# Sums of weight blocks: from VectorE in the down-projection to accumulating DMAs in DRAM

## The chip, the core and the metric

The kernel runs on one core of a Trainium2 chip. A core has five engines that work side by side, each through its own queue in order: PE (TensorE, matrix products), PEld (the weight loads of PE, which overlap its products), DVE (VectorE), ACT (ScalarE) and POOL (GpSimd); SP (SyncE) computes nothing and issues most of the DMAs. Sixteen DMA engines move data between DRAM (HBM) and the on-chip memory SBUF, or from DRAM to DRAM. Products land in PSUM, from where ACT or DVE copy them out. Engines wait for each other and for DMAs by semaphores.

The metric is the device time of one execution in microseconds (us); lower is better.

## What is computed

One step of a one-layer encoder on 1056 rows (1024 prompt rows and 32 sample rows) of 1024 features, all in float32. Cut to what matters:

```python
def layer(x, p, attend, conv_buf, g_mix, w_in, conv_w, w_attn_out, w_conv_out, w_o,
          g_ffn, w_up, w_down, g_ple, w_ple_gate, w_ple):
    h = rmsnorm(x, g_mix)
    proj = h @ w_in                                   # 1024 -> 5120: the input stage
    q, k, v, cb, cc, cx, ga, gc = jnp.split(proj, SPLITS, axis=-1)
    y_attn = attend(q, k, v).reshape(b, t, SB_WIDTH) @ w_attn_out
    conv_out, new_buf = causal_conv(cc * cx, conv_buf, conv_w)
    y_conv = (cb * conv_out) @ w_conv_out
    merged = jax.nn.sigmoid(ga) * y_attn + jax.nn.sigmoid(gc) * y_conv
    x = x + merged @ w_o
    f = jnp.square(jax.nn.relu(rmsnorm(x, g_ffn) @ w_up)) @ w_down    # up, then down
    x = x + f
    x = x + jax.nn.sigmoid(rmsnorm(x, g_ple) @ w_ple_gate) * (p @ w_ple)
```

`w_down` is 4096 x 1024. The change touches how its blocks are prepared.

## The kernel before

**Stages.** The work runs in order: input projection (from the start to about 429 us), attention with small projections filled in, branch outputs and `w_o`, up-projection (to about 1075 us), down-projection (about 1075 to 1405 us), and the gate of the per-layer embedding with the final norm. Activations are held with features on the 128 partitions and rows along the free dimension.

**Products.** Every float32 operand is split into a high part, rounded to the float32r format of TensorE, and the low remainder; a product is three matmuls (high by high, high by low, low by high). The high part of a weight block is a cast on ACT, the low part a subtraction on DVE.

**Seven products in place of eight.** The large projections use the Strassen-Winograd scheme on 2 x 2 blocks: from the weight blocks A11, A12, A21, A22 come S1 = A21 + A22, S2 = S1 - A11, S3 = A11 - A21 and S4 = A12 - S2; from the activation blocks come T1 to T4; seven block products and some additions of results give the four output blocks.

**The input stage.** After the first gates, which use plain products, sets of two output blocks are worked on in pairs (`seven_pair`, 25 steps of 12 or more matmuls each, eight pairs). Between steps, `run` lets every generator in the list `side` advance once: these load the weights of the next sets (SP queue, four buffers), sum their blocks on POOL (`prepare`, L228, and `prepare_inner`), cast the high parts on ACT (L167), subtract the low parts on DVE (L226), and finish the results of earlier sets (scales, sigmoids, stores to DRAM). ACT copies most products out of PSUM: the copies named `u_i` (L491), `s_i` (L486) and `p_i` (L481) must be made before PE can go on in the same PSUM bank. The order on ACT, PE, DVE and POOL is the order in which the code issues the instructions. `after(n, ...)` holds a generator back for n steps.

**The down-projection.** 56 units: two halves c of the 4096 inputs, in each the seven products P1, P2, P5, P6, P7, P4, P3 in that order, in each product four column pairs n2. One unit is 48 matmuls. Weights come as 128 x 1024 blocks (0.5 MB) by SP (`fetch_w`, L1704) three units ahead; activation operands by `fetch_mid` six units ahead. `sum_w` makes S1 (P5), S2 (P6), S3 (P7) and S4 (P3) on DVE two units ahead of their use: at L1732 for P5 and P6, at L1727 for P7, at L1730 for P3; P1, P2 and P4 use blocks of `w_down` as they are. For S1 and S3 two blocks are loaded instead of one (the second into the tile `sw` for P5, into a second `raw_dn` buffer for P7). S1 is kept in `sw` and turned into S2 and then used for S4. `high_w` (ACT, L1737) and `low_w` (DVE, L1743) then split the block. The products of a unit are L1850 to L1852; DVE and ACT add them out of PSUM at L1854 to L1864.

Of the kernel before, what the change touches and what calls it, by code (L numbers as in the profile page):

```python
# [9 lines left out]
F32 = mybir.dt.float32  # L10
# [5 lines left out]
P = 128  # L16
D = 1024
KD = D // P
SEQ = 1024
DEC = 32  # L20
T = SEQ + DEC
# [19 lines left out]
RAW_GATES = 6  # L41
ORDER = "LSAFBFG"
LAG = 2
START = 0.33
BP = (8, 9)
TAIL = 0
# [5 lines left out]
def tile_step(  # L52
# [8 lines left out]
    nc = tc.nc  # L61
# [3 lines left out]
    wraw = ctx.enter_context(tc.tile_pool(name="wraw", bufs=RB))  # L65
    wsp = ctx.enter_context(tc.tile_pool(name="wsp", bufs=2))
    dpool = ctx.enter_context(tc.tile_pool(name="dpool", bufs=1, space=bass.MemoryType.DRAM))

    def blk(name, dt=F32, shape=None):
        return bpool.tile(shape or [P, T], dt, tag="B", name=name)  # L70
# [58 lines left out]
    add, sub = ALU.add, ALU.subtract  # L129
    dve, pool = nc.vector.tensor_tensor, nc.gpsimd.tensor_tensor  # L130
    raws, ws, side = {}, {}, []
# [428 lines left out]
    def after(n, *gens):  # L560
        for _ in range(n):
            yield
        for g in gens:
            yield from g

    def call(f, *a):
        f(*a)
        yield
# [187 lines left out]
    NSET = DFF // (2 * P)  # L756
    NCH = 2
    NP_ = NSET // NCH
# [11 lines left out]
    cvd = dpool.tile([4, 2, P, T], F32, name="cvd")  # L770
    ed = dpool.tile([KD, P, T], F32, name="ed")
    edt = dpool.tile([P, 2, 2 * P], F32, name="edt")
    oT = []
    ch, cl = [], []
    st, cst = {}, {}
# [534 lines left out]
    with tc.manual_schedule(engines=MM):  # L1310
        nc.scalar.preload_act_table_set("sqrt_and_others")
        run(first_gates())
        side.append(after(1, stats_x()))
        side.extend(ahead_of("i", 3, 3))
        side.append(after(5, inner_operands("x", gmix, lambda to, f: nc.sync.dma_start(to, xf[f][:, :TH]))))
        m = blk("m1_i2"), blk("m2_i2")
        run(seven("i2", *m, copy_of))
        follow(*SETS[2], m)
        last_ = len(SETS) - 1
        for a in range(3, last_, 2):  # L1320
            more = a + 2 < last_
            pair_side("i", a, a + 1, in_pair(a + 2, a + 3) if more else None)
            if not more:
                side.extend([after(15, low_parts()), after(8, call(fetch_in, last_)), after(12, prepare(f"i{last_}", (6, 8, 10, 12, 15, 17)))])
            run(input_pair(a, a + 1))
        m = blk(f"m1_i{last_}"), blk(f"m2_i{last_}")
        side.append(after(2, call(p_fetch), call(keys_values, 0, 0), call(queries, 0, 0, 0), call(queries, 0, 0, 1), call(queries, 0, 0, 2), call(queries, 0, 0, 3)))
        side.append(after(8, *(call(p_parts, f) for f in range(2)), *(call(embed_weights, i) for i in range(2))))
        side.append(after(9, call(next, work)))
        run(seven(f"i{last_}", *m, copy_of))  # L1330
        follow(*SETS[last_], m)
        run(ahead(START))
        while side:
            run(range(1))
# [68 lines left out]
    def pace():  # L1403
# [6 lines left out]
        load, own = [], []  # L1410
        for n in range(ns + LAG):
            a, b, c = size(n - 1), size(n - LAG), size(n - LAG - 1)
# [15 lines left out]
    with tc.manual_schedule(engines=MM):  # L1428
        next(sample)
        for n in range(len(steps) + LAG + 1):  # L1430
            done_f, parts = 0, None
            w0, w1 = (pace_ + [FILL])[n : n + 2]
            if n < len(steps):
                i = steps[n][2]
# [8 lines left out]
            for op in ORDER:  # L1443
# [9 lines left out]
                elif op == "G" and n > LAG and steps[n - LAG - 1][2] % 2 == 1:  # L1453
                    p, j, i_ = steps[n - LAG - 1]
# [231 lines left out]
    def up_source(a, b):  # L1686
# [3 lines left out]
    SEVEN = (  # L1690
        ("P1", "A11", "B11"), ("P2", "A12", "B21"), ("P5", "S1", "T1"), ("P6", "S2", "T2"),
        ("P7", "S3", "T3"), ("P4", "A22", "T4"), ("P3", "S4", "B22"),
    )
    ND = NCH * 7 * 4
    dws, opd, mraw, sw, dt_ = {}, {}, {}, {}, {}

    def unit(u):
        c, r = divmod(u, 28)
        i, n2 = divmod(r, 4)
        return c, i, n2  # L1700

    def quarter_w(to, a, b, c, n2):
        n = 2 * n2 + a
        nc.sync.dma_start(to, w_down[n, b][:, c * NP_ : (c + 1) * NP_, :])  # L1704

    def fetch_w(u):
        c, i, n2 = unit(u)
        k = SEVEN[i][0]
        raw = dws[u] = wraw.tile([P, NP_, P], F32, tag="raw", name=f"raw_dn{u}")
        a, b = {"P2": (0, 1), "P5": (1, 1), "P4": (1, 1), "P3": (0, 1)}.get(k, (0, 0))  # L1710
        quarter_w(raw, a, b, c, n2)
        if k == "P5":
            sw[n2] = swp.tile([P, T], F32, tag="sw", name=f"sw{u}")
            quarter_w(sw[n2][:, : NP_ * P].rearrange("p (k n) -> p k n", n=P), 1, 0, c, n2)
        elif k == "P7":
            dws[u] = raw, wraw.tile([P, NP_, P], F32, tag="raw", name=f"raw_dn{u}b")
            quarter_w(dws[u][1], 1, 0, c, n2)

    def sum_w(u):

        c, i, n2 = unit(u)
        k, raw = SEVEN[i][0], dws[u]
        if k in ("P1", "P4", "P2"):
            return
        s = sw[n2][:, : NP_ * P].rearrange("p (k n) -> p k n", n=P)
        if k == "P7":
            dve(raw[0], raw[0], raw[1], op=sub)  # L1727
            dws[u] = raw[0]
        elif k == "P3":
            dve(raw, s, raw, op=sub)  # L1730
        else:
            dve(s, s, raw, op=add if k == "P5" else sub)  # L1732
            dws[u] = s

    def high_w(u):
        hi = wsp.tile([P, NP_, P], F32R, tag="whi", name=f"whi_dn{u}")
# [32 lines left out]
    def held(k, n2):  # L1769
        return dt_[k][n2 // 2][:, n2 % 2, :]  # L1770
# [57 lines left out]
    def down_unit(u):  # L1828
        c, i, n2 = unit(u)
        k = SEVEN[i][0]  # L1830
        hi, lo = dws.pop(u)
        ops = [opd[(c * 7 + i) * 4 + j] for j in range(NP_ // 2)]
        e = None

        ends = {"P2": (0, 0), "P7": (1, 1), "P4": (1, 0), "P3": (0, 1)}.get(k)
        if ends:
            n, h = 2 * n2 + ends[0], ends[1]
            e = fetch_x(c, n, h)
        if k in ("P1", "P5", "P6"):
            d = state({"P1": "b1", "P5": "b5", "P6": "b6"}[k], n2)  # L1840
        elif k in ("P2", "P7"):
            d = dp.tile([P, TH], F32, tag="e", name=f"c{u}", bufs=EB)
        else:
            d = held({"P4": "b6", "P3": "b5"}[k], n2)
        for t in range(2):
            ps = group(f"ps_dn{u}_{t}", TQ)
            q = quarters[t]
            for j in range(NP_):
                oh, ol = (o[:, j % 2, q] for o in ops[j // 2])
                nc.tensor.matmul(ps, hi[:, j, :], oh, start=j == 0, stop=False)  # L1850
                nc.tensor.matmul(ps, hi[:, j, :], ol, start=False, stop=False)  # L1851
                nc.tensor.matmul(ps, lo[:, j, :], oh, start=False, stop=j == NP_ - 1)  # L1852
            if k in ("P1", "P5"):
                nc.scalar.copy(d[:, q], ps)  # L1854
            elif k in ("P2", "P6"):
                dve(d[:, q], ps, held("b1", n2)[:, q], op=add)
            elif k == "P7":
                b6 = held("b6", n2)[:, q]
                dve(d[:, q], ps, held("b5", n2)[:, q], op=add)  # L1859
                dve(b6, ps, b6, op=add)  # L1860
            elif k == "P4":
                dve(d[:, q], ps, d[:, q], op=add)
            else:
                dve(d[:, q], d[:, q], ps, op=sub)  # L1864
            yield
        if k == "P6":
            b5 = held("b5", n2)
            later.append(partial(dve, b5, d, b5, op=sub))
        if ends:
            into_x(c, n, h, d, e)  # L1870
# [261 lines left out]
    with tc.manual_schedule(engines=MM):  # L2132
# [36 lines left out]
        swp = ctx.enter_context(tc.tile_pool(name="swp", bufs=4))  # L2169
# [4 lines left out]
        for u in range(ND):  # L2174
            v = u + 4
            if u + 1 < ND:
                high_w(u + 1)
            else:
                ple_high(0)
            if v < ND:  # L2180
                high_mid(v)
            if u + 2 < ND:
                sum_w(u + 2)
            if u + 1 < ND:
                low_w(u + 1)
            else:
                ple_low(0)
            body = down_unit(u)
            if u + 3 < ND:
                fetch_w(u + 3)  # L2190
            else:
                ple_fetch(u + 3 - ND)
            if v + 2 < ND:
                fetch_mid(v + 2)
            if u == LASTP:
                nc.scalar.preload_act_table_set("sqrt_and_others")
                later.extend(partial(norm_late, n, halves[0]) for n in (1, 3, 5, 7, 0, 2, 4, 6))
                seen["rs3"], seen["ssq3"] = blk("rs3"), blk("ssq3")
            settle(2 + (u < ND - 1) if u >= LASTP else 1)
            next(body)  # L2200
            if v < ND:
                low_mid(v)
            settle(2 + (u < ND - 1) if u >= LASTP else 1)
            for _ in body:
                pass
# [9 lines left out]
        for t in (1, 2):  # L2215
            ps = rows_of([seen["ssq2"][:, tt[t]]], t, f"ps_n{t}")
# [109 lines left out]
```

## Time and profile before

| | |
|---|---|
| median of 3 runs | 1518.92 us (1518.25 to 1519.84) |
| the profiled execution | 1519.13 us |
| its span, from the first to the last instruction | 1517.4 us |
| granted TensorE clock, mean of the span | 0.998 of full speed |
| busy: PE, PEld, DVE, ACT, POOL | 99%, 98%, 76%, 52%, 28% of the span |
| moved by DMA | 270.47 MB, mean 178 GB/s |

How to read the views that follow: a group of instructions is given by line, engine, operation, the tiles it writes and reads (`out<-in`), its shape and count, then its busy time in us, the mean of one in ns and the idle time of the engine just before. A row of waits says which instruction of which engine waited for which other, in total, how often, and the longest, all in us. A row of a stretch gives its length and for each engine the busy us in it (and how many instructions), the granted clock, the share of the 16 DMA engines that was busy and the rate. A row by tile has least, median and most ns, and the first and the last start in us. Matmuls are pipelined and their ends are modelled. Idle time of an engine that is not the bottleneck costs nothing.

### The profile page before, as it was taken

The page shows a single profiled execution, that of the slowest core. Times are in us where ns is not written, and L with a number is a line of the kernel's source. Part 1 is how long each engine was busy: PE and PEld are TensorE (multiplying, and loading weights), DVE is VectorE, ACT ScalarE, POOL GpSimd, SP SyncE. Part 2 cuts the span into 40 slices and gives each one's busy share as a digit, 9 for nine tenths or more (in the row PEclk, how much of TensorE's full clock was granted, in tenths as well). Part 3 has the DMA queues.
Part 4 walks back from the last instruction along what each step waited for, and adds up shares of the span by engine and source line. Part 5 has one row for each costly group of instructions (what it writes and reads, how often), then busy time and mean ns, then how long its engine had stood idle before and what let it go on. Part 6 is the DMA issues. An engine that isn't in the chain of part 4 may idle for free.

```text
span 1517.4 us, 29531 instructions
## 1 busy us (share of the span) xinstructions
PE 1496.5 (99%) x11600; PEld 1483.4 (98%) x11600; DVE 1154.7 (76%) x1567; ACT 785.1 (52%) x1549; POOL 430.7 (28%) x362
## 2 busy tenths in 40 slices
PE   8999999999999999999999999999999999999997
PEld 8999999999999999999999999999999999999997
DVE  7667688879578989876786586666687977789856
ACT  6654444445467667433475555555543334444656
POOL 1233334444121211003324343332020221012453
PEclk9999999999999999999999999999999999999999
DMA  6624425422677432545644434444986897583443
GB/s 244 211 71 169 163 63 197 155 84 96 221 254 249 131 110 78 208 173 193 230 139 156 143 130 147 145 154 160 349 282 203 270 336 250 192 276 106 147 131 114
DMA packets 116746, 270.47 MB, mean 178 GB/s; under 512 B 14048, under 2 KB 30048, under 8 KB 116608
## 3 DMA queue, kind: packets, MB, share of 16 engines
q1 hardware_dynamic: 115888, 266.40, 51.9%
q8 instruction: 91, 1.49, 0.4%
q10 hardware_dynamic: 720, 2.19, 0.4%
q14 instruction: 47, 0.39, 0.1%
HBM read 187.81 MB, written 80.73 MB: 177 GB/s over the span
## 4 chain that ended last, share of the span: by engine, by line
PE 93%; DVE 3%; ACT 2%; issue 1%; DMA 1%; SPq 0%; DVEq 0%; ACTq 0%
PE ps_dn L1852 7%; PE ps_dn L1851 7%; PE ps_dn L1850 7%; PE ps_A11i L347 4%; PE ps_A11i L348 4%; PE ps_A11i L349 4%; PE ps_A11u L348 4%; PE ps_A11u L347 4%; PE ps_A11u L349 4%; PE av L1199 2%; PE ps_wo L111 2%; PE ps_wo L110 2%; PE ps_wo L109 2%; PE ps_S1i L348 2%; PE ps_S1i L349 2%; PE ps_S1i L347 2%
## 5 line engine op out<-in xcount | busy, mean ns | idle before, releaser
L1852 PE MATMUL ps_dn<-fh,wlo_dn 128*128 128x264 f32 x896 | 255.2, 285 | 0.0
L1851 PE MATMUL ps_dn<-fl,whi_dn 128*128 128x264 f32 x896 | 254.7, 284 | 0.2 <-DVE fl L1759 0.2
L1850 PE MATMUL ps_dn<-fh,whi_dn 128*128 128x264 f32 x896 | 254.8, 284 | 0.0
L1851 PEld LDWEIGHTS ps_dn<-fl,whi_dn 128*128 128x128 f32 x896 | 168.6, 188 | 0.4 <-DVE fl L1759 0.4
L1852 PEld LDWEIGHTS ps_dn<-fh,wlo_dn 128*128 128x128 f32 x896 | 168.5, 188 | 0.2 <-DVE wlo_dn L1743 0.2
L1850 PEld LDWEIGHTS ps_dn<-fh,whi_dn 128*128 128x128 f32 x896 | 168.7, 188 | 0.0
L1792 POOL TENSOR_TENSOR c<-c,ssq 128x528 f32<-128x528 f32 x16 | 26.4, 1652 | 242.6 <-DVE c L1859 122.5
L1737 ACT CAST whi_dn<-raw_dn 128x1024 fp32r<-128x1024 f32 x40 | 42.1, 1052 | 94.0 <-PE ps_dn L1851 79.7
L1144 DVE TENSOR_TENSOR_SCAN r<-r 128x128 f32<-128x128 f32 (+3 forms) x64 | 86.7, 1355 | 4.8 <-POOL r L1137 4.8
L1743 DVE TENSOR_TENSOR wlo_dn<-raw_dn,whi_dn 128x1024 fp32r<-128x1024 f32 x40 | 71.0, 1776 | 24.0 <-ACT whi_dn L1737 23.5
L347 PE MATMUL ps_A11i<-T,shS_i 128*128 128x264 f32 x288 | 82.5, 287 | 1.6 <-ACT u_i L491 1.6
L348 PE MATMUL ps_A11i<-T,shS_i 128*128 128x264 f32 x288 | 82.1, 285 | 0.0
L349 PE MATMUL ps_A11i<-T,slS_i 128*128 128x264 f32 x288 | 81.9, 284 | 0.0
L1137 POOL TENSOR_SCALAR_AFFINE_SELECT r<-r 128x128 f32<-128x128 f32 x64 | 34.1, 533 | 139.6 <-ACT r L1130 139.5
L347 PE MATMUL ps_A11u<-T,shS_u 128*128 128x264 f32 x256 | 73.1, 286 | 0.0
L348 PE MATMUL ps_A11u<-T,shS_u 128*128 128x264 f32 x256 | 72.9, 285 | 0.0
L349 PE MATMUL ps_A11u<-T,slS_u 128*128 128x264 f32 x256 | 72.8, 285 | 0.0
L1759 DVE TENSOR_TENSOR fl<-mr,fh 128x1056 fp32r<-128x1056 f32 x56 | 69.7, 1247 | 3.8 <-ACT fh L1754 3.8
L1754 ACT CAST fh<-mr 128x1056 fp32r<-128x1056 f32 x56 | 59.9, 1074 | 5.8 <-DMA mr<-mdB 5.8
L111 PE MATMUL ps_wo<-mh,wlo_wo 128*128 128x352 f32 x192 | 62.1, 323 | 0.0
L110 PE MATMUL ps_wo<-ml,whi_wo 128*128 128x352 f32 x192 | 62.0, 323 | 0.0
L109 PE MATMUL ps_wo<-mh,whi_wo 128*128 128x352 f32 x192 | 61.5, 323 | 0.0
(1652 smaller groups left out, 5622.6 us busy)
## 6 DMA issues: line engine op xcount, KB each, us to landing
raw_dn<-in_w_down_dram SPq DMA_DIRECT2D x56, 512.0 KB, 4.9
mr<-mdT SPq DMA_DIRECT2D x32, 528.0 KB, 5.6
mdB<-m SPq DMA_DIRECT2D x48, 264.0 KB, 2.1
mr<-mdB SPq DMA_DIRECT2D x24, 528.0 KB, 6.6
s<-gd SPq DMA_DIRECT2D x16, 528.0 KB, 5.2
mdT<-ta SPq DMA_DIRECT2D x32, 264.0 KB, 3.2
raw_pg<-in_w_ple_gate_dram SPq DMA_DIRECT2D x15, 512.0 KB, 3.5
gd<-m_i SPq DMA_DIRECT2D x12, 528.0 KB, 3.0
```

What stands on the lines that cost most here:

```text
L109: nc.tensor.matmul(ps, wh, xh[k][:, cols], start=(k == order[0]), stop=False)
L110: nc.tensor.matmul(ps, wh, xl[k][:, cols], start=False, stop=False)
L111: nc.tensor.matmul(ps, wl, xh[k][:, cols], start=False, stop=(k == order[-1]))
L347: nc.tensor.matmul(p_, wh[:, k, :], h, start=new and n == 0, stop=False, **on)
L348: nc.tensor.matmul(p_, wh[:, k, :], l, start=False, stop=False, **on)
L349: nc.tensor.matmul(p_, wl[:, k, :], h, start=False, stop=z, **on)
L1144: nc.vector.tensor_tensor_scan(rev, rev, rev, 1.0, ALU.mult, ALU.bypass)
L1743: dve(lo, raw, hi.bitcast(F32), op=sub)
L1759: dve(l, mraw.pop(v), opd[v].bitcast(F32), op=sub)
L1850: nc.tensor.matmul(ps, hi[:, j, :], oh, start=j == 0, stop=False)
L1851: nc.tensor.matmul(ps, hi[:, j, :], ol, start=False, stop=False)
L1852: nc.tensor.matmul(ps, lo[:, j, :], oh, start=False, stop=j == NP_ - 1)
```

## The change

The four sums of blocks of `w_down` are made in DRAM, in 16 new tensors `dsum` of 1 MiB (four sums by four column pairs, both halves c at once). A generator `down_sums` joins the list `side` after the first gates and starts 16 steps later. For each column pair it copies a block of `w_down` into the tensor, DRAM to DRAM, by a DMA that ACT issues, and adds another block, or an earlier sum, by an accumulating DMA that POOL issues. [...] Between copy and addition lie 8 steps, in all 40 steps for a column pair and 160 for four; one column pair is worked on after the other.

In the down-projection `sum_w` and its 32 subtractions and additions are gone, and so are the second loads for P5 and P7 (16 loads of 0.5 MB); `fetch_w` reads the finished sum for P5, P6, P7 and P3.

```diff
+SPACE = 8
+DS0 = 16
...
+    dsum = {k: [dpool.tile([P, NSET, P], F32, name=f"ds{k}{n}") for n in range(KD // 2)] for k in ("S1", "S2", "S3", "S4")}
+
+    def down_sums():
+
+        def copy(k, n, a, b):
+            nc.scalar.dma_start(dsum[k][n], w_down[2 * n + a, b])
+
+        def plus(k, n, src):
+            nc.gpsimd.dma_start(dsum[k][n], src, accum_op=add, max_dma_last_dim=4096)
+
+        for n in range(KD // 2):
+            copy("S1", n, 1, 0)
+            yield from after(SPACE)
+            copy("S3", n, 0, 0)
+            plus("S1", n, w_down[2 * n + 1, 1])
+            yield from after(SPACE)
+            copy("S2", n, 0, 0)
+            plus("S3", n, w_down[2 * n + 1, 0])
+            yield from after(SPACE)
+            copy("S4", n, 0, 1)
+            plus("S2", n, dsum["S1"][n])
+            yield from after(2 * SPACE)
+            plus("S4", n, dsum["S2"][n])
...
         side.append(after(5, inner_operands("x", gmix, lambda to, f: nc.sync.dma_start(to, xf[f][:, :TH]))))
+        side.append(after(DS0, down_sums()))
         m = blk("m1_i2"), blk("m2_i2")
...
     def fetch_w(u):
         c, i, n2 = unit(u)
-        k = SEVEN[i][0]
+        k = SEVEN[i][1]
         raw = dws[u] = wraw.tile([P, NP_, P], F32, tag="raw", name=f"raw_dn{u}")
-        a, b = {"P2": (0, 1), "P5": (1, 1), "P4": (1, 1), "P3": (0, 1)}.get(k, (0, 0))
-        quarter_w(raw, a, b, c, n2)
-        if k == "P5":
-            sw[n2] = swp.tile([P, T], F32, tag="sw", name=f"sw{u}")
-            quarter_w(sw[n2][:, : NP_ * P].rearrange("p (k n) -> p k n", n=P), 1, 0, c, n2)
-        elif k == "P7":
-            dws[u] = raw, wraw.tile([P, NP_, P], F32, tag="raw", name=f"raw_dn{u}b")
-            quarter_w(dws[u][1], 1, 0, c, n2)
-
-    def sum_w(u):
-        ...
+        src = dsum[k][n2] if k in dsum else w_down[2 * n2 + int(k[1]) - 1, int(k[2]) - 1]
+        nc.sync.dma_start(raw, src[:, c * NP_ : (c + 1) * NP_, :])
...
             elif k in ("P2", "P6"):
-                dve(d[:, q], ps, held("b1", n2)[:, q], op=add)
+                dve(d[:, q], ps, held("b1", n2)[:, q], op=add if k == "P2" else sub)
             elif k == "P7":
                 b6 = held("b6", n2)[:, q]
-                dve(d[:, q], ps, held("b5", n2)[:, q], op=add)
-                dve(b6, ps, b6, op=add)
+                dve(d[:, q], held("b5", n2)[:, q], ps, op=sub)
+                dve(b6, b6, ps, op=sub)
...
             else:
-                dve(d[:, q], d[:, q], ps, op=sub)
+                dve(d[:, q], ps, d[:, q], op=sub)
...
-            if u + 2 < ND:
-                sum_w(u + 2)
```

More of the change, by code (lines that the diff above doesn't have):

```diff
@@ L1694, in tile_step @@
     ND = NCH * 7 * 4
-    dws, opd, mraw, sw, dt_ = {}, {}, {}, {}, {}
+    dws, opd, mraw, dt_ = {}, {}, {}, {}
     def unit(u):
@@ L1700, in unit @@
         return c, i, n2
-    def quarter_w(to, a, b, c, n2):
-        n = 2 * n2 + a
-        nc.sync.dma_start(to, w_down[n, b][:, c * NP_ : (c + 1) * NP_, :])
     def fetch_w(u):
         c, i, n2 = unit(u)
-        k = SEVEN[i][0]
+        k = SEVEN[i][1]
         raw = dws[u] = wraw.tile([P, NP_, P], F32, tag="raw", name=f"raw_dn{u}")
-        a, b = {"P2": (0, 1), "P5": (1, 1), "P4": (1, 1), "P3": (0, 1)}.get(k, (0, 0))
-        quarter_w(raw, a, b, c, n2)
-        if k == "P5":
-            sw[n2] = swp.tile([P, T], F32, tag="sw", name=f"sw{u}")
-            quarter_w(sw[n2][:, : NP_ * P].rearrange("p (k n) -> p k n", n=P), 1, 0, c, n2)
-        elif k == "P7":
-            dws[u] = raw, wraw.tile([P, NP_, P], F32, tag="raw", name=f"raw_dn{u}b")
-            quarter_w(dws[u][1], 1, 0, c, n2)
-    def sum_w(u):
[L1721 to L1733, printed above, removed]
+        src = dsum[k][n2] if k in dsum else w_down[2 * n2 + int(k[1]) - 1, int(k[2]) - 1]
+        nc.sync.dma_start(raw, src[:, c * NP_ : (c + 1) * NP_, :])
     def high_w(u):
```

## The prediction

> **What bounds the kernel now.** I read the page first (busy shares, the chain that ended last), then the stretches of the down-projection, then what PE waits for there, then the sums themselves. From the page:
>
> ```profile
> span 1517.4 us, 29531 instructions
> PE 1496.5 (99%) x11600; PEld 1483.4 (98%) x11600; DVE 1154.7 (76%) x1567; ACT 785.1 (52%) x1549; POOL 430.7 (28%) x362
> PE 93%; DVE 3%; ACT 2%; issue 1%; DMA 1%; SPq 0%; DVEq 0%; ACTq 0%
> ```
>
> PE is busy 99% of the span and 93% of the chain that ended last; DVE has 3%. The change gives DVE time back, so the question is whether PE waits for DVE where the sums are made. The stretches (length, then busy us by engine, clock, DMA share, GB/s):
>
> ```profile
> 1075.00:1180.00 105.00, 104.83 (x859) 104.41 (x858) 78.76 (x84) 44.70 (x58) 9.39 (x5) 1.00 0.80 273
> 1180.00:1300.00 120.00, 120.00 (x985) 120.00 (x984) 97.60 (x105) 47.12 (x56) 25.94 (x15) 1.00 0.81 277
> 1300.00:1405.00 105.00, 105.00 (x859) 104.88 (x859) 92.34 (x111) 44.58 (x54) 19.28 (x11) 1.00 0.59 191
> ```
>
> PE is idle for 105.00 - 104.83 = 0.17 us in 330 us of down-projection. DVE is busy there 78.76 + 97.60 + 92.34 = 268.7 us, 81%, below its limit. The waits of PE from 1060 to 1420 us are one row, and the sums lie here:
>
> ```profile
> PE ps_dn L1851 <- DVE fl L1759: 0.2, 1, 0.2
> ...
> L1732 DVE TENSOR_TENSOR sw<-sw,raw_dn x16: 1206/1216/1221, 1112.0 to 1316.9; 128x1024 f32<-128x1024 f32 x16
> L1730 DVE TENSOR_TENSOR raw_dn<-sw,raw_dn x8: 1209/1215/1218, 1205.4 to 1388.5; 128x1024 f32<-128x1024 f32 x8
> L1727 DVE TENSOR_TENSOR raw_dn<-raw_dn,raw_dn16b x1: 1217/1217/1217, 1158.8 to 1158.8; 128x1024 f32<-128x1024 f32 x1
> ...
> L1727 DVE TENSOR_TENSOR raw_dn<-raw_dn,raw_dn47b x1: 2306/2306/2306, 1340.7 to 1340.7; 128x1024 f32<-128x1024 f32 x1
> ```
>
> That wait is for `fl`, an operand of the activations, not for a sum. In the Trainium skill, "Perfetto Trace Analysis", section Identifying the Most-Contended Engine, the busy time of matmuls is no measure of headroom, because they are pipelined, and that of weight loads is to be used. By that rule the headroom of the stage is the idle time of PEld, 330 - 104.41 - 120.00 - 104.88 = 0.7 us instead of 0.17 us; the verdict is the same and the bound four times as wide.
>
> **The change, part by part.** *The sums leave DVE.* 16 at L1732 by 1.216 us, 8 at L1730 by 1.215 us, 8 at L1727 between 1.217 and 2.306 us: 39 to 48 us of DVE work. None of it is on PE's path, and the first sum starts at 1112.0 us. What is late next is the split of the block: DVE waits for ACT's high part (`wlo_dn`, below), and PE for neither. Gain taken: 0; at most 0.7 us. Does the rate of the matmuls suffer from DVE's traffic? The stretch 1084 to 1108 us holds no sum; 1160 to 1184 us holds those of P7 (three of the four L1727). Their matmuls and loads:
>
> ```profile
> DVE wlo_dn L1743 <- ACT whi_dn L1737: 28.9, 20, 3.5
> ...
> 1084.00:1108.00 24.00, 24.00 (x199) 24.00 (x198) 0.87 (x2) 2.94 (x8) 1.00 1.00 378
> 1160.00:1184.00 24.00, 24.00 (x200) 24.00 (x199) 4.76 (x12) 0.00 (x0) 1.00 0.75 240
> ```
>
> 199 against 200 in 24 us, so no.
>
> *The 16 second loads go, and the other sums are read where blocks were.* SP issues 16 loads of 0.5 MB less; four `raw` buffers are then ahead for P7 too. PE waits for no load in this stage, so 0. The exchanged signs cost 0: the same instructions.
>
> *When the new DMAs are issued.* The copies `s_i` (L486) mark the steps: four to a pair, the first at step 3 of the first pair, the last at step 17 of the eighth, 7 x 25 + 14 = 189 steps apart.
>
> ```profile
> L486 ACT COPY s_i<-ps_S1i x32: 373/380/383, 84.1 to 395.2; 128x264 f32<-128x264 f32 x32
> ```
>
> One step is (395.2 - 84.1) / 189 = 1.65 us. The generator starts after 16 of them, of which the set before the pairs takes 14, so the first copy is issued at step 3 of the first pair, 84 us, and the last addition 160 steps later, at 348 us, 80 us before the stage ends. All of it is spread over 264 us; 8 steps are 13.2 us.
>
> *ACT's 16 issues.* ACT issues four DMAs in this stage already:
>
> ```profile
> L914 ACTq DMA_DIRECT2D cvd<-cvh x4: 326/326/327, 235.7 to 367.9; - x4
> L914 ACTq EVENT_SEMAPHORE  x2: 17/17/17, 233.8 to 357.2; - x2
> ...
> 78.00:120.50 42.50, 41.74 (x341) 41.27 (x340) 27.66 (x54) 20.38 (x47) 14.93 (x13) 1.00 0.19 64
> 161.00:203.00 42.00, 42.00 (x348) 41.97 (x347) 31.75 (x46) 18.30 (x49) 16.07 (x13) 1.00 0.36 127
> ...
> PE ps_A11i L347 <- ACT u_i L491: 1.2, 2, 0.8
> ACT u_i L491 <- PE ps_A11i L349: 10.7, 16, 1.1
> ```
>
> 16 x 0.326 = 5.2 us of ACT, which is busy 18 to 20 us in the 41 us of a pair. It is hidden where ACT waits for PE. The tight place is `u_i`: before 16 of these copies (80 to 350 us) ACT waits 10.7 / 16 = 0.67 us on average and 1.1 us at most, and twice it was PE that waited, 1.2 us in all. One of these is in the first pair, where PE is idle 0.76 us of 42.5, and the first copy stands right ahead of it, so its 0.33 us goes to PE. The other 15 fit the gaps. Cost: 0.3 us; bounds 0 and 5.2.
>
> *POOL's 16 issues.* No DMA of POOL's is in this trace. The nearest rows are ACT's issue, 0.33 us, and POOL's longest sum of this stage, 2.2 us (below): 5 to 35 us in 16 pieces. I take 1 us each, nearer the issue, whose kind it is. Queued behind are POOL's sums for the next sets. How early they are shows in one load:
>
> ```profile
> L228 POOL TENSOR_TENSOR s_i<-s_i,raw_i11o x2: 2155/2172/2189, 229.7 to 250.1; 128x512 f32<-128x512 f32 x2
> ...
> L91 SPq DMA_DIRECT2D raw_i9r<-in_w_in_dram x1: 333/333/333, 168.0 to 168.0; - x1
> L228 POOL TENSOR_TENSOR raw_i9r<-raw_i9r x1: 1293/1293/1293, 184.3 to 184.3; 128x512 f32<-128x512 f32 x1
> L167 ACT CAST shS_i<-raw_i9r x1: 626/626/626, 196.5 to 196.5; 128x512 fp32r<-128x512 f32 x1
> DMA to landing us min/median/max: 3.4/3.4/3.4
> ```
>
> The sum is ready at 185.6 us and cast at 196.5: 10.9 us to spare. An issue costs PE 0, even at 2.2 us. An addition also waits for its copy, issued 13.2 us before; POOL stands only if a copy takes longer than that, and its sums are late only at 13.2 + 10.9 us.
>
> *The traffic.* A tensor has 128 x 2048 x 4 bytes = 1.05 MB. Rows:
>
> ```profile
> q1 hardware_dynamic: 13523, 32.59, 35.0%
> mdB<-m SPq DMA_DIRECT2D x48, 264.0 KB, 2.1
> raw_dn<-in_w_down_dram SPq DMA_DIRECT2D x56, 512.0 KB, 4.9
> DMA to landing us min/median/max: 3.2/4.9/8.7
> DVE m_i L499 <- DMA kd<-kh: 1.3, 1, 1.3
> ```
>
> The fullest stretch above, 1084 to 1108 us, moved 378 GB/s at a share of 1.00; at that rate 1.05 MB take 2.8 us of all 16 engines, and 264 KB (0.27 MB) 0.7 us, so 1.4 us of the 2.1 us to landing are fixed. No row shows a copy DRAM to DRAM or an addition. Lower end for both: each byte passes once, 2.8 + 1.4 = 4.2 us. Upper end: every read and write counts apart, 5.6 us of engines for a copy, 8.3 us for an addition (two reads, one write), 7.0 and 9.7 us to landing. I take the lower end for the copy, whose bytes pass the engine once as a load's do, and two passes, 5.6 us, for the addition, which must read both operands. That is 16 x (2.8 + 5.6) = 134 us of engines in 264 us, a share of 0.51 on top of the 0.35 of 80 to 350 us (row q1): 0.86. At the lower ends it is 0.69, at the upper ones 0.35 + 16 x 13.9 / 264 = 1.19.
>
> In the Trainium skill, "DMA: Bandwidth & Descriptors", section Latency and other measured facts, copies between HBM tensors ran at 207 to 214 GB/s. By that figure a copy would take an estimated 5.1 us of engines and my share would be 1.0 in place of 0.86; no row here shows it.
>
> What a share of that size does to loads the down-projection shows: at 0.80 its 0.5 MB blocks land in 4.9 us in the median and 8.7 at worst, where `raw_i9r` took 3.4. So loads come 1.5 us later, at worst 5.3, against 10.9 to spare: 0. One place has nothing to spare: DVE's `m_i` at L499 waited 1.3 us for the store `kd`, whose buffer it needed. A landing 1.5 us later holds DVE 1.5 us longer with PSUM copies behind it; PE does not wait there today. I charge 0.5 us; bounds 0 and 5.3.
>
> **The sum** against the profiled execution, 1519.13 us (span 1517.4 and 1.7 around it): -0 + 0.3 + 0 + 0.5 = +0.8, 1519.9. That execution is 0.2 above the median 1518.92, so for the median 1519.7 us. A difference within 0.2% (3.0 us) is about what a measurement of this kernel cannot tell from none. What lies around the span may grow by a queue that POOL opens; no row tells, and 0 to another 1.7 us bounds it.
>
> **Rivals.** *ACT stands in front of its copies (slower).* Two of the four DMAs of ACT have a semaphore wait ahead of them (row above). If that is because ACT's and SP's transfers report their landing on the same few semaphores in turn, a copy must wait until the last transfer on its semaphore has landed. A wait for a landing of 3.4 to 4.9 us, against a gap of 0.67 us before `u_i`, leaves 2.7 to 4.2 us to PE when it strikes there. One struck copy is about the 3.0 us of the bound, so it decides from two of the 16 on: with the 0.8 us above +6 to +9, 1525 to 1528, say 1526. For it: ACT has 16 such issues where it had four. Against: those two waits took 17 ns.
>
> *The DMA engines are full (slower).* At the upper ends the share is 1.19 and a copy with its addition keeps the engines 13.9 us; a load behind them lands in 3.4 + 13.9 = 17 us, some 3 us beyond the 10.9 to spare. Each of the 13 sets (two in each 41 us of the 264) would then lose up to 3 us: +10 to +39, say +13 us, 1532. It decides from (1 - 0.35) x 264 / 16 = 10.7 us of engines for a copy and its addition on, that is 7.9 us for the addition. Against: it must run at under 36% of the rate of a load.
>
> *The matmuls gain from a quieter DVE (faster).* If they became 1% quicker, 330 us would give 3.3 us: 1515.6. The two stretches above, 199 and 200 in 24 us, speak against it.
>
> **Chances.** No change, with the sum above: 0.62; its own range 1518.2 (0.7 gained, nothing lost) to 1522. ACT in front of its copies: 0.18. Full engines: 0.14. Quicker matmuls: 0.06. Slower by over 0.2% takes the two rivals and a little of the first case's upper end: 0.34; within 0.2%: 0.60; faster: 0.06. The range leaves out the faster rival and the worse part of the full engines: 1517.8 to 1527.5.
>
> **What would show it.** Right: DVE in 1075 to 1405 us falls by some 40 us, PE there stays at 329.8 or more; from 84 to 348 us the DMA share is about 0.86, PE waits for `u_i` grow from 1.2 to about 1.5 us, new waits of PE stay under 1 us, and the raw loads land within 9 us. Wrong: `u_i` with long waits for semaphores ahead of the new DMAs; POOL rows waiting for copies for over 13 us; L228 or L167 waiting for loads; an addition that takes longer than 9.7 us to land; or a longer time around an unchanged span.

## The result, and the profile after

The changed kernel takes 1543.76 us (median of 4 runs, 1541.63 to 1545.18) against 1519.2 us for the kernel before on the same chip: 24.6 us more, ratio 1.0160 with a 95% interval of 1.0147 to 1.0173. The forecast was 1519.7 us, with 1527.5 as the upper end of its range. The profiled execution of the changed kernel took 1545.18 us; its span is 26.1 us longer than that of before. Lines of the code moved by two: what was L478 to L499 in the profile before is L480 to L501 now. The sums of the changed kernel have S2 = S1 + A11, S3 = A11 + A21 and S4 = A12 + S2, as if the first row of blocks of the weight were negated; the additions out of PSUM take the sign back, by the same instructions with add and subtract exchanged.

From the page of the changed kernel, the span and the busy times:

```profile
span 1543.5 us, 29539 instructions
PE 1506.1 (98%) x11600; PEld 1491.7 (97%) x11600; DVE 1120.9 (73%) x1535; ACT 785.2 (51%) x1549; POOL 434.8 (28%) x378
```

DVE's busy time fell by 1154.7 - 1120.9 = 33.8 us. PE is *busier* by 9.6 us with the same 11600 matmuls, so some of them ran slower; the other 26.1 - 9.6 = 16.5 us are idle time. The down-projection, in stretches shifted by 26 us so that they begin at the same work as the three of before:

```profile
1101.00:1206.00 105.00, 104.83 (x860) 104.44 (x859) 66.22 (x74) 44.63 (x58) 6.68 (x5) 1.00 0.74 247
1206.00:1326.00 120.00, 120.00 (x985) 120.00 (x984) 84.51 (x94) 47.12 (x56) 20.00 (x15) 1.00 0.78 254
1326.00:1431.00 105.00, 105.00 (x860) 105.00 (x859) 80.04 (x102) 45.94 (x56) 17.05 (x11) 1.00 0.52 166
```

DVE has 230.8 us there in place of 268.7, 38 us less. PE is busy 329.83 us as before, and does 860 + 985 + 860 = 2705 matmuls in place of 859 + 985 + 859 = 2703: nothing gained, nothing lost. Nearly all of the difference lies in the input stage. Its stretches (length, busy us by engine with the count of instructions, clock, DMA share, GB/s), first of the kernel before, then of the changed one:

```profile
80.00:117.00 37.00, 36.24 (x296) 35.77 (x295) 22.92 (x48) 16.35 (x38) 13.23 (x12) 1.00 0.21 67
117.00:141.00 24.00, 24.00 (x199) 24.00 (x198) 18.45 (x24) 12.87 (x28) 7.30 (x4) 1.00 0.64 243
141.00:350.00 209.00, 208.52 (x1714) 208.25 (x1713) 166.49 (x229) 94.02 (x226) 85.77 (x62) 1.00 0.36 123
```

```profile
80.00:117.00 37.00, 36.24 (x296) 35.76 (x295) 23.61 (x47) 17.32 (x40) 15.62 (x14) 1.00 0.64 187
117.00:141.00 24.00, 21.99 (x181) 21.78 (x179) 13.34 (x18) 12.49 (x27) 7.02 (x5) 1.00 0.94 293
141.00:350.00 209.00, 194.62 (x1524) 192.85 (x1525) 153.13 (x205) 82.14 (x197) 92.33 (x68) 0.96 0.82 241
```

The count of matmuls is the plainest measure of a loss: at full rate 199 take 24 us, 0.1206 us each. From 141 to 350 us 190 fewer were done, 22.9 us; from 80 to 141 us 18 fewer, 2.2 us; together 25.1 of the 26.1 us. (In short stretches the DMA share can pass 1.00: the times of packets then overlap on an engine, so a time of the DMA engines here is the time that packets took, not that of an engine of its own.) Who was late is in the waits of the changed kernel, first the rows of PE over the whole span that bear on this, then of DVE and ACT from 80 to 380 us:

```profile
PE pt_v L892 <- DVE dv L876: 5.9, 2, 3.4
PE ps_A11i L349 <- ACT u_i L493: 4.5, 3, 2.9
PE ps_A11i L349 <- DVE m_i L480: 3.9, 3, 2.9
PE ps_inA12i5y L334 <- DVE m_i L501: 2.4, 1, 2.4
...
PE ps_dn L1851 <- DVE fl L1759: 0.2, 1, 0.2
```

```profile
ACT dv L877 <- DMA vd<-vs: 15.7, 2, 8.3
...
DVE dv L876 <- DMA vd<-vs: 14.1, 2, 7.5
...
DVE m_i L480 <- DMA out_v_out_dram<-m_i: 6.6, 1, 6.6
...
DVE m_i L501 <- DMA kd<-kh: 5.4, 1, 5.4
...
ACT kh L856 <- DMA cvd<-cvh: 3.7, 1, 3.7
```

PE waits for DVE and ACT, and these wait for *stores*. `dv`, `m_i` and the stored `vs`, `kh` all come from one pool of 37 buffers (`blk`); a new tile is given a buffer whose last content is still on its way to DRAM. Each of PE's five idle times of 2.4 us or more stands behind one of these waits: at 141 us `kd`, at 191 and 325 us `vd`, at 265 us `cvd`, at 340 us `out_v`. In the kernel before, from 80 to 380 us, the only such rows were `kd<-kh` with 1.3 us, which is 5.4 us now, and `qd<-qh` with 0.3 us. Loads landed later as well, `raw_i13r` after 12.8 us where it took 5.6 (the forecast's sign was 9), but neither PE nor ACT nor DVE waited for one. The stores land later while the DMA engines are busier (from 60 to 440 us, median us from issue to landing; before, then after):

```profile
out_v_out_dram<-m_i SPq DMA_DIRECT2D x4, 528.0 KB, 3.7
vd<-vs SPq DMA_DIRECT2D x16, 256.0 KB, 2.5
kd<-kh SPq DMA_DIRECT2D x4, 512.0 KB, 5.5
```

```profile
q0 software_dynamic: 4352, 16.78, 24.0%
q10 hardware_dynamic: 1088, 18.94, 14.0%
...
dsS<-in_w_down_dram POOLq DMA_DIRECT2D x8, 1024.0 KB, 13.4
dsS<-dsS POOLq DMA_DIRECT2D x8, 1024.0 KB, 11.7
...
vd<-vs SPq DMA_DIRECT2D x16, 256.0 KB, 6.5
...
out_v_out_dram<-m_i SPq DMA_DIRECT2D x4, 528.0 KB, 10.9
...
kd<-kh SPq DMA_DIRECT2D x4, 512.0 KB, 10.1
```

The slower matmuls follow four of these five idle times. PE's timeline of the changed kernel at the first (start, us, line, tiles, idle before), and a short stretch behind each of the five:

```profile
141.39 0.39 PE L334 MATMUL ps_inA12i5y<-B,whi_i5y 128*128 128x264 f32 x1 [2.40 <-DVE m_i L501]
...
142.35 0.29 PE L350 MATMUL ps_A11i<-T,shA_i 128*128 128x264 f32 x1
142.47 0.32 PE L351 MATMUL ps_A11i<-T,slA_i 128*128 128x264 f32 x1
142.60 0.42 PE L349 MATMUL ps_A11i<-T,shA_i 128*128 128x264 f32 x1
142.81 0.42 PE L350 MATMUL ps_A11i<-T,shA_i 128*128 128x264 f32 x1
```

```profile
142.00:146.00 4.00, 4.00 (x23) 4.00 (x22) 3.30 (x6) 0.38 (x1) 0.00 (x0) 0.57 0.74 270
265.00:269.00 4.00, 3.71 (x18) 3.71 (x19) 3.64 (x4) 2.53 (x6) 2.20 (x2) 0.57 1.52 570
324.00:328.00 4.00, 3.38 (x16) 3.41 (x17) 3.45 (x8) 2.59 (x9) 0.00 (x0) 0.50 1.42 404
340.00:344.00 4.00, 4.00 (x23) 4.00 (x22) 3.75 (x3) 1.72 (x4) 3.29 (x3) 0.57 0.70 233
191.00:195.00 4.00, 3.68 (x31) 3.71 (x32) 3.49 (x9) 2.60 (x9) 0.00 (x0) 1.00 0.91 317
```

After 2.40 us of idling the matmuls start every 0.12 us at first, then from 142.6 to about 145.9 us every 0.22 us, then every 0.12 us again: some 15 matmuls at 0.10 us extra, 1.5 us on top of the 2.4. The granted clock of 142 to 146 us is 0.57 (23 matmuls in place of 33), and that of 141 to 350 us is 0.96. Behind the idle times of 2.86 us at 265, 3.44 us at 325 and 2.89 us at 340 us it is 0.57, 0.50 and 0.57; the slow stretches there begin 0 to 1.0 us after the first matmul and last 3.5, about 5 and 3.3 us. By the spacing of the matmuls the four together cost an estimated 7 of the 9.6 us. An idle time of 2.50 us at 191 us was followed by no such drop: the last stretch has 1.00. In the Trainium skill, "TensorE: Matmul & The Clock Gate", Part 1, the clock falls to half after an idle window of some 3.4 us, and the window runs freely. Three of the slow stretches are about that long, but drops after only 2.40, 2.86 and 2.89 us of idling are not what the Trainium skill states.

### The profile page after: what moved, and what is told of

It is laid out like the page before. It is cut to its first block, busy times and chain, and to the rows that moved or that the text cites. A ratio compares the mean times of both kernels' runs of the same rounds, so it can differ in the third digit from the quotient of the medians.

```text
span 1543.5 us, 29539 instructions
## 1 busy us (share of the span) xinstructions
PE 1506.1 (98%) x11600; PEld 1491.7 (97%) x11600; DVE 1120.9 (73%) x1535; ACT 785.2 (51%) x1549; POOL 434.8 (28%) x378
## 4 chain that ended last, share of the span: by engine, by line
PE 67%; DVE 4%; issue 1%; POOL 1%; ACT 1%; DMA 0%; DVEq 0%; POOLq 0%; SPq 0%; ACTq 0%
PE ps_dn L1852 7%; PE ps_dn L1851 7%; PE ps_dn L1850 7%; PE ps_A11u L350 4%; PE ps_A11u L349 4%; PE ps_A11u L351 4%; PE av L1224 2%; PE ps_wo L113 2%; PE ps_wo L112 2%; PE ps_wo L111 2%; PE ps_S1u L350 2%; PE ps_S1u L349 2%; PE ps_S1u L351 2%; PE pa L1205 2%; PE ps_pg L111 1%
## 5 line engine op out<-in xcount | busy, mean ns | idle before, releaser
L1743 DVE TENSOR_TENSOR wlo_dn<-raw_dn,whi_dn 128x1024 fp32r<-128x1024 f32 x56 | 89.8, 1604 | 62.3 <-ACT whi_dn L1737 61.7
L1737 ACT CAST whi_dn<-raw_dn 128x1024 fp32r<-128x1024 f32 x56 | 58.9, 1051 | 125.3 <-PE ps_dn L1851 103.8
L1792 POOL TENSOR_TENSOR c<-c,ssq 128x528 f32<-128x528 f32 x16 | 21.4, 1336 | 247.6 <-DVE c L1859 125.3
L349 PEld LDWEIGHTS ps_A11i<-T,shS_i 128*128 128x128 f32 x288 | 55.3, 192 | 9.9 <-ACT u_i L493 5.1
## 6 DMA issues: line engine op xcount, KB each, us to landing
dsS<-in_w_down_dram POOLq DMA_DIRECT2D x8, 1024.0 KB, 13.4
```

The costliest lines, as they stand in the source:

```text
L349: nc.tensor.matmul(p_, wh[:, k, :], h, start=new and n == 0, stop=False, **on)
L1743: dve(lo, raw, hi.bitcast(F32), op=sub)
```

## The experiments

The edits are shown against the changed kernel. All runs are compared with the kernel before on the same chip.

**Each half alone.** The new reading of `w_down` without any sums made (the edit below), and the kernel before with `down_sums` added, its sums still made on DVE as well.

```diff
-        side.append(after(DS0, down_sums()))
...
-        src = dsum[k][n2] if k in dsum else w_down[...]
+        src = w_down[2 * n2 + int(k[1]) % 2, int(k[1]) // 3] if k in dsum else w_down[...]
```

> The down side of the change alone: no sums are made and no new DMA is issued in the input stage; where a sum would be read, a block of w_down as it is is read in its place, so this kernel leaves out the sums S1 to S4. Theory (the whole loss comes from the new traffic in the input stage, and the down-projection gains nothing because PE never waited for the sums): 1518.5 to 1519.5 us, DVE some 40 us less busy, PE idle in the down-projection unchanged at 0.2 us. Rival (the relief of DVE gives a gain that the loss hid): under 1516 us.

Measured: 1519.28 us, ratio 0.9997 (0.9988 to 1.0006). The time of DVE that is freed in the down-projection is worth nothing within that interval.

> The input side alone: the 32 new DMAs as in the changed kernel, but the down-projection makes its sums on VectorE as before and does not read the new tensors. Theory (all of the loss is in the input stage): 1541 to 1546 us. Rival (reading the sums back, or the order of the loads in the down-projection, costs something too): under 1538 us.

Measured: 1545.05 us, ratio 1.0166 (1.0151 to 1.0182), with the same rows of waits (`ACT dv <- vd<-vs` 14.9 us, `DVE m_i <- out_v` 5.9 us). The whole loss is that of the 32 DMAs in the input stage.

**Copies without additions, and plain writes in place of additions.**

```diff
-            nc.gpsimd.dma_start(dsum[k][n], src, accum_op=add, max_dma_last_dim=4096)
+            pass                                                            # copies only
+            nc.gpsimd.dma_start(dsum[k][n], src, max_dma_last_dim=4096)     # plain
```

> The 16 copies that ACT issues stay, the 16 additions that POOL issues are left out (the tensors hold copies, so the sums are left out). Theory (traffic makes stores land late, and engines then wait for the buffers): a copy keeps the engines about 3 us and an addition about 5.7, so a third of the traffic is left; 1520 to 1527 us, with PE waits behind late stores under 5 us. Rival (ACT's issues and their semaphore waits hold the copies out of PSUM): 1535 us or more, since all 16 are still there.

Measured: 1520.66 us, ratio 1.0008 (0.9999 to 1.0017). From 80 to 350 us, and the queue of the copies from 60 to 440 us:

```profile
80.00:350.00 270.00, 268.44 (x2197) 267.25 (x2196) 210.06 (x300) 124.25 (x293) 107.79 (x76) 1.00 0.57 189
```

```profile
q10 hardware_dynamic: 1088, 18.94, 15.2%
```

At a share of 0.57 the landings have begun to grow (`kd<-kh` from 5.5 to 8.0 us), but PE is busy 268.44 us where it was 36.24 + 24.00 + 208.52 = 268.76 before. ACT issues all its 16 copies here and PE loses nothing; with stores that land less late, this alone does not clear ACT's place in front of them, to which the last runs below come back.

> The 16 DMAs that POOL issues stay with their waits and their pieces of 4 KB, but write instead of adding (the sums are left out). Theory (traffic): POOL's DMAs land in 7 to 9 us where the additions took 12 to 14, the DMA share between 80 and 350 us falls from 0.81 to about 0.66, and the time to 1525 to 1535 us. Rival (POOL stands at its DMAs, in issue and in waits, and its sums for the next sets come late): 1541 us or more, since POOL issues and waits as before.

Measured: 1532.45 us, ratio 1.0080 (1.0064 to 1.0096), the share 0.70: half of the loss, within the range of the theory. The queue of the plain writes has 13.2% of the engines' time in 380 us, 3.1 us for each write, where the additions have 24.0%, 5.7 us. The waits are the same kind (`ACT dv <- vd<-vs` 15.3 us, `DVE m_i <- kd<-kh` 9.2 us). So the accumulation costs almost as much again as the write, and half the loss comes without it.

**The same plain traffic, but issued by ACT.**

```diff
-            nc.gpsimd.dma_start(dsum[k][n], src, accum_op=add, max_dma_last_dim=4096)
+            nc.scalar.dma_start(dcopy[k][n], w_down[2 * n, 1] if k in ("S2", "S4") else src)
```

> In place of each addition that POOL issues, ACT issues a second plain copy of 1 MB into another tensor, which waits for nothing; the additions, and so the sums, are left out. Theory (traffic on the engines, whoever issues it): share about 0.7 and landings as with the plain DMAs of POOL, 1524 to 1534 us. Rival (POOL's queue or its software DMAs are what hurts): 1519 to 1522 us, no more than with the copies alone.

Measured: 1528.86 us, ratio 1.0065 (1.0046 to 1.0085), share 0.69. With no DMA on POOL at all, 9.6 us are lost, near the 13.2 us of the plain writes from POOL. The executions of the two overlap (1527.3 to 1533.8 and 1527.2 to 1533.8 us), so it is the traffic, and no difference between the issuing engines is shown.

**The same bytes in smaller pieces, and at half the rate.** Quarters of 256 KB every two steps; and two column pairs in this stage, two in the up-projection, 16 steps apart.

```diff
+        parts = [slice(32 * i, 32 * i + 32) for i in range(4)]   # quarters
...
-SPACE = 8
+SPACE = 16                                                       # half rate
-        for n in range(KD // 2):
+        for n in ns:
...
+        side.append(after(DS0, down_sums((0, 1))))
+        side.append(after(DS0, down_sums((2, 3))))               # up-projection
```

> All sums are made, but each copy and each addition is cut into four pieces of 256 KB, two steps apart: the same bytes, spread evenly. If a store is late because it stands behind one long copy and one long addition at a time, the waits shorten: 1524 to 1534 us. If the mean share of the engines decides: 1538 to 1546 us. POOL issues 64 times 0.9 us instead of 16 times, 43 us more of POOL's time; if that counts, over 1546 us.

Measured: 1549.53 us, ratio 1.0196 (1.0180 to 1.0212): worse, and in the range that was set for POOL's issues. But from 80 to 380 us ACT and DVE wait for no sum of POOL's. `kd` lands after 11.6 us in the median, and one wait of DVE for it reached 8.5 us. ACT, with 64 issues, also stood 6.9 us in front of one copy, at 275.4 us, until a store `kd` had landed. Smaller pieces gave the stores no better place; how the loss divides among these is not shown.

> All sums are made, at half the rate (16 steps between copy and addition): two column pairs in the input stage and two in the up-projection. A copy and an addition then stand together half as often per time, and the share between 80 and 350 us falls from 0.81 to about 0.6. Theory (late stores): the input stage keeps about half of its stores late, 8 to 14 us of loss there; in the up-projection the share rises from 0.46 to about 0.7, and the stores of its results are as many, so 2 to 10 us there: 1530 to 1542 us. Rival (only a nearly full set of engines hurts): 1519 to 1525 us.

Measured: 1555.08 us, ratio 1.0241 (1.0206 to 1.0276): worst of all, and outside both ranges. The profiled execution is its slowest, 1563.45 us. From 80 to 350 us the share is 0.57, as with the copies alone, but PE does 136 matmuls fewer than before (16.4 us), and a single wait for a store costs it 6.3 us there. The larger part of the loss comes later; in the up-projection, from 640 to 1100 us:

```profile
DVE tb L1662 <- DMA mdT<-m: 32.2, 4, 8.6
```

It is again a store that DVE waits for, another one in another stage (6.2 us in the kernel before); PE waits 17.0 us there for `slS_u`, which DVE makes behind it. The mean share is thus no measure of the loss. That it depends on which large transfer is under way when a store with little slack is issued would fit, but no run shows it alone.

**Where the sums are put.** Half of the sums (the rest read as raw blocks), five steps apart, in the pairs with few stores and in those with many.

```diff
-SPACE = 8
+SPACE = 5
...
+        side.append(after(89, down_sums(0)))    # few stores; 64 and 139 for many
+        side.append(after(164, down_sums(1)))
```

> Only the sums of two of the four column pairs are made (for the other two a block of w_down is read as it is, so half of the sums is left out), each within one pair of sets of the input stage (steps 5 apart in place of 8, so denser than in the changed kernel): in the fourth pair (about 203 to 244 us) and the seventh (326 to 367), where SP stores few results. Theory (the loss is made by stores of results that land late and hold buffers): few stores, little loss, 1519 to 1523 us, with PE waits under 2 us in the two stretches. Rival (the share of the DMA engines alone makes loads late): 0.25 + 0.8 is over 1, so 1527 us or more.

Measured: 1534.52 us, ratio 1.0097 (1.0080 to 1.0113). From 80 to 380 us:

```profile
POOL dsS L783 <- issue: 30.7, 3, 12.8
...
DVE m_i L480 <- DMA out_conv_out_dram<-m_i: 8.2, 2, 5.3
...
ACT shS_i L169 <- POOL raw_i17r L230: 4.6, 1, 4.6
```

> The same DMAs as in the run with few stores, the same two column pairs and spacing (the same half of the sums left out), but in the third pair (161 to 203 us) and the sixth (285 to 326), where SP stores values, queries and keys. Theory (late stores hold buffers): 1526 to 1536 us, with DVE and ACT waiting for the stores vd and v_out for 5 us or more at a time, and PE behind them. Rival (the share alone): within 3 us of the run with few stores.

Measured: 1528.12 us, ratio 1.0061 (1.0046 to 1.0076), with `ACT dv <- vd<-vs` 12.6 us and `DVE m_i <- out_v` 7.3 us. The order is the reverse of what the theory of the stores gives by their number: by its own ranges the first run went to the rival. The traces show two things that the theory left out. Even the tiny store of `conv_out` holds a buffer of the pool and lands late, after up to 12.0 us. And with five steps between a copy and its addition POOL stands before its addition for up to 12.8 us, with the sums of the next weights queued behind; ACT then waits for those. In the changed kernel POOL stands too, 24.2 us in four waits, the longest 8.9 us, but its sums are not late for it: ACT's only wait for POOL from 80 to 380 us lasts 0.9 us (up to 1.2 us before). How much of the first run's loss each of the two makes is not shown.

**Stores that hold no buffer.** Every large store of the stage reads a resident operand tile; the results are not stored. Done to the changed kernel and to the kernel before.

```diff
+    def fixed(n=T):
+        return oper["B11"][0].bitcast(F32).rearrange("p a t -> p (a t)")[:, :n]
...
-            nc.sync.dma_start(k_out[p], m)
+            nc.sync.dma_start(k_out[p], fixed())
```

> All DMAs of the changed kernel stay, with their sizes and destinations, but the stores of results in the input stage (gates, keys, queries, values, the convolution, the outputs k, v and conv) read one operand tile that stays in place for the whole stage, in place of the tile with the result. So the results are not stored and the outputs are not the reference's; the traffic is the same, and no buffer waits for a late store. Theory (late stores hold buffers, DVE and ACT stand for them in order, PE behind): 1519 to 1524 us, at a DMA share between 80 and 350 us of still about 0.8. Rival (late loads, or POOL standing at its DMAs): 1535 us or more.

Measured: 1540.46 us, ratio 1.0133 (1.0111 to 1.0154), in the rival's range.

> The kernel before with the same exchange of the stores' source (the results are not stored), as the measure for the run above. Both theories: 1516 to 1520 us, since PE waits for only 1.2 us behind ACT between 80 and 350 us.

Measured: 1525.63 us, ratio 1.0039 (1.0024 to 1.0054). This is outside its range of 1516 to 1520 us. The difference of the pair is 14.8 us in place of 24.6, which decides little: the exchange itself costs 6 us (with a gap of PE of 3.4 us at 77 us, ahead of the first copy), and the stall of PE of 6.4 us at 130 us in the first of the pair is of a kind that the changed kernel doesn't have. A guess was that SP, which no longer waits for results, runs ahead with its stores and crowds the queue. So the exchange was made once more with SP's pace kept:

```diff
+        paced("DVE", m[:1, T - 2 :])        # two elements to a private tile, stored by a DMA of 8 bytes
+        nc.sync.dma_start(k_out[p], fixed())
```

> The changed kernel with all its copies and additions; as in the run with the fixed source the stores of results read a resident operand, so that they hold no buffer (the results are not stored), but now two elements of each finished result are first copied to a private tile and stored by a DMA of 8 bytes right ahead of the big store, so that SP issues each big store no sooner than in the changed kernel. To be read against the kernel before with the same exchange, run beside it. Theory (stores that land late hold the buffers): the difference between the two is 0 to 5 us, DVE and ACT wait for no store in the input stage. Rival (loads, ACT's and POOL's places in their queues, or the matmuls themselves suffer as well): a difference of 10 us or more with PE waiting for casts or sums of loaded blocks.

> The kernel before with the same exchange (fixed source, 8 bytes of each finished result stored ahead of each big store). Both theories: within 4 us of before, 1517 to 1523 us; the gap of 3.4 us at 77 us of the run with the fixed source alone goes, since SP is paced again.

Measured: 1539.88 us, ratio 1.0142 (1.0121 to 1.0163), and 1524.35 us, ratio 1.0034 (1.0021 to 1.0046), the second outside its range of 1517 to 1523 us. The gap at 77 us did not go (2.3 us in the second of the pair), so the guess about SP does not explain it, and it remains open. The pair differs by 15.5 us, where the theory gave 0 to 5, and PE's longest wait is for a cast: by the letter of the expectation the rival has it. The stretches show where the difference lies. They are of the changed kernel with the exchange, then of the kernel before with it:

```profile
117.00:141.00 24.00, 15.84 (x114) 15.40 (x114) 9.92 (x16) 7.90 (x17) 8.81 (x9) 0.86 1.03 295
141.00:350.00 209.00, 206.03 (x1688) 205.30 (x1687) 164.96 (x251) 94.04 (x230) 101.65 (x75) 1.00 0.73 208
```

```profile
117.00:141.00 24.00, 24.00 (x199) 24.00 (x198) 19.84 (x28) 14.10 (x33) 9.73 (x7) 1.00 0.74 249
141.00:350.00 209.00, 208.53 (x1713) 208.26 (x1713) 169.56 (x260) 94.10 (x231) 85.72 (x60) 1.00 0.20 67
```

From 141 to 350 us, where the changed kernel lost 190 matmuls (22.9 us), 25 are lost with stores that hold no buffer, 3.0 us, though all copies and additions run and the share is still 0.73. DVE and ACT wait for no store's buffer there; PE, ACT and DVE wait for no loaded weight block from 80 to 380 us in this run or in the changed kernel. So in this stretch most of the loss is that of the buffers. The rest of the pair's difference is mainly one place, 85 matmuls or 10.3 us from 117 to 141 us. ACT's timeline there:

```profile
118.00 0.38 ACT L493 COPY u_i<-ps_A11i 128x264 f32<-128x264 f32 x1 [0.55 <-PE ps_A11i L351]
130.76 0.51 ACTq L780 DMA_DIRECT2D dsS<-in_w_down_dram  x1
131.32 0.62 ACT L169 CAST shA_i<-raw_i4r 128x512 fp32r<-128x512 f32 x1 [12.94 <-DMA vd<-B]
```

ACT stands in front of its third copy until the store `vd`, which shares no data with the copy, has landed, and a cast that PE needs is queued behind; PE then waits 8.2 us. In front of the fourth copy ACT stands another 3.5 us, for a store `qd`. In the changed kernel eight of the sixteen copies name a semaphore to wait for in the trace's records too, but ACT has no such wait in the rows of its stage: the third is issued at 112.0 us, right after its `u_i`, and the cast behind it follows at 112.54. So this loss belongs to the exchange and not to the changed kernel, by the two traces; no run has the exchange without it.

What stays open: the exchange also freed buffers sooner, so how much of the 22.9 us each single store is worth was not told apart; nor was it shown what a pool with more buffers does.

## Why the prediction was wrong

**What held.** The sums leave DVE for a gain of 0: the wait of PE in the down-projection is the same 0.2 us, and that half alone gives a ratio of 0.9997. The price of the new DMAs was near: 1.0 us was taken for POOL's issue and 0.90 measured; ACT's issue took 0.50 us where 0.326 was taken from smaller DMAs, 8 us in 16 and still hidden, by the run with copies alone (PE's waits for `u_i` from 60 to 440 us are 1.8 us there, before 1.6). A copy took (14.0 - 1.4)% of 380 us over 16, that is 3.0 us of the engines (2.8 forecast; 1.4% is the share of ACT's four old stores), and an addition 5.7 us (5.6 forecast). Both forecasts came from a choice of how often each byte passes, which no run tests, so that they came this near is in part luck. The share of 80 to 350 us was 0.81 (0.86 forecast). The 207 to 214 GB/s of the Trainium skill ("DMA: Bandwidth & Descriptors", Latency and other measured facts), which the forecast set beside its own price, would make an estimated 5.1 us of a copy; the Trainium skill gives them for tensors with a row pitch of 512 KiB, or with a padded one, and the copies here have rows of 8 KiB one behind the other. The measured 3.0 to 3.3 us are some 320 to 350 GB/s.

**The step that failed** is the last of the traffic: "So loads come 1.5 us later, at worst 5.3, against 10.9 to spare: 0. One place has nothing to spare", charged with 0.5 us and bounded by 5.3. Three things were wrong in it.

First the size: the extra landing time was read from blocks of 0.5 MB in the down-projection at a share of 0.80. Here, at 0.81, the median landing of a store grew by 4.0 (`vd`), 4.6 (`kd`) and 7.2 us (`out_v`), and single ones by more: one store `cvd` took 10.3 us where the median was 2.6. The additions themselves landed after 11.7 to 13.4 us in the median, beyond the bound of 9.7. In the down-projection loads of one size follow each other, and here stores stand among copies and additions of 1 MiB; whether that makes the difference is not shown, and pieces of 256 KB did not help.

Second the count: the slack was looked up for the loads, in a single row, and for stores the one wait that the trace of before showed, 1.3 us for `kd<-kh`, was taken as the only place without slack (the same trace had `qd<-qh` with 0.3 us). A wait that is not there in the trace says only that the slack is above zero. With the later landings `vd`, `out_v` and `cvd` came to hold buffers as well, in waits of up to 8.3 us, and `kd` for longer. PE's idle time grew by 16.5 us, where 0.5 us had been charged.

Third what an idle PE costs: 9.6 of the 26.1 us are slower matmuls, most of them at the lower clock behind four gaps. The forecast had the granted clock in its rows, 1.00 everywhere, and no term for it.

**The rivals.** *Full engines* was the nearest, with its 1532 us and 0.14; but it decided from 10.7 us of engines for a copy and its addition, which took 8.7, and it went by late loads, which cost PE nothing. The time was lost below its threshold, by stores. *ACT in front of its copies* did not happen in the changed kernel (no such wait in its trace; copies alone 1.0008), but it is real: the paced exchange shows 12.9 us of it, the quarters 6.9. *Quicker matmuls* is refuted by the down-projection, with 2705 matmuls in 330 us against 2703, and by that half alone.

## What to carry to other kernels

Before adding DMA traffic to a stage that is bound by PE, list the buffers that *stores* hold and ask for each who needs it next and how early the store has landed; a landing that is 5 us later is free for a prefetched load and not for a ring of result buffers. A share of the DMA engines that leaves room on average is not enough: at the same 0.57 one run lost 1.4 us and another 16.4 us in this stage alone. And a gap of PE can cost more than its length: behind four of the five gaps of 2.4 us or more the clock was halved for 3.3 us or longer.

## What was not expected of the hardware

- An accumulating DMA DRAM to DRAM took 5.7 us of the 16 engines for 1.05 MB where a plain one from the same queue took 3.1, and its issue kept POOL 0.90 us where the plain one took 0.57:

```profile
L783 POOL DMA_DIRECT2D dsS<-in_w_down_dram x8: 875/897/1074, 89.0 to 319.5; - x8
```

```profile
L783 POOL DMA_DIRECT2D dsS<-in_w_down_dram x8: 572/573/747, 89.7 to 307.8; - x8
```

(the changed kernel, then the plain writes).

- The lower clock began 0 to 1.2 us after the first matmul behind an idle time and lasted 3.3 to about 5 us; an idle time of 2.50 us had none, one of 2.40 us did.
- A copy issued by ACT waited 12.9 us for the landing of a store of SP's that shares no data with it (11.1 us in the run without pacing). The forecast had this as a rival, with waits of 3.4 to 4.9 us.
